# An encoder trunk on one core: a fourteenth seven-product pair in each half of the down-projection, a fifth pair with stored weight sums, and smaller stored activation sums

## The chip, the cores and the metric

The kernel runs on 1 core of one Trainium2 chip. The metric is the device time of one execution in microseconds (us). A core has engines that run beside each other: PE (TensorE, matrix products; PEld is its weight loads), DVE (VectorE), ACT (ScalarE), POOL (GpSimd, here mostly an issuer of DMAs) and SP (SyncE, an issuer of DMAs). Each engine works through its own instructions in order and waits on semaphores for the others.

## The reference

`x` is 256 positions by 2048 columns, all in float32. A mixer (a gated MLP branch and a neighbourhood attention branch) comes first and is not touched here. Then comes the part that matters:

```python
def conv_ffn(x, g_norm, w_up, conv_k, conv_b, w_down):
    h = rms_norm(x, g_norm)
    up = h @ w_up                       # 2048 -> 2 * 5504
    ...
    gate, val = jnp.split(up, 2, axis=-1)
    return x + (jax.nn.silu(gate) * val) @ w_down     # 5504 -> 2048
```

followed by a last `rms_norm`.

## The kernel before

**Products.** A float32 product is made of three matmuls on operands split in a high and a low part (`triple`, L316 to L319: high times high, low times high, high times low). The weights come from memory in pieces (`wraw`, five buffers, loads on SP's queue at L145). ACT copies a piece to its high part (`whi`, L170) and DVE subtracts to get the low part (`wlo`, L171); four buffers each, so this runs at most some three pieces ahead of PE.

**Up.** The stage has 22 groups (here numbered 0 to 21). A group makes two blocks of 128 gate columns and the two matching value columns, in eight pieces; group 21 has one block of each. After a group, DVE and ACT add the bank halves (L1066, L1068), run the convolution and the gate (L1074 to L1087) and split the result into the activation tiles `ff["a"]`, a few pieces later, within the next group. Group f makes activation pair f: two blocks of 128 of the 5504 columns.

**Down.** It is done in two halves of 1024 output columns (`g_dn`, `wide` and `run_wide`). A half takes 43 pieces of 128 rows: 21 pairs and one single. A plain piece is four triples, so a pair is eight. For the pairs of `DOWN_QUADS` the eight are replaced by seven, in Strassen's manner: these need four blocks of sums of the activations (`act_blocks`: s3, n1, p2, s4) and sums of the weights. In the first step of such a pair run three triples, which need of the sums only the last block s4; in the second step run four, which need the other three blocks and the weight sums.

The activation sums are made once, in the group behind their own (`sums`, `sums_split`), written to memory by POOL from the tile `so`, and loaded by POOL (`stored`) before each half needs them. The weight sums are made by DVE and ACT when the pair comes (`weight_sums`, `weight_sums_split`), except for the pairs of `DOWN_SPLIT`: theirs are made in the up stage by a job (`split_ahead`: one load `tw`, four additions at L1298, two splits at L1303 and L1304, four writes) and loaded as four tiles h13, l13, h24, l24 (`split_read`, L1258). Such a pair's first piece needs only half its columns. A job that starts with group g adds in the last two pieces of group g and the first two of group g+1 and splits in group g+1.

**Order.** The order on each engine is written out by hand: `at(i, f)` puts f in front of piece i. The second argument pair of a split pair, (6, 6), says how many pieces ahead its loads are put. Inside `wide` that loop uses the name `lead`, so that after the first split pair of a half the activation sums of later pairs are put 6 pieces ahead, not 4.

Of the kernel before, what the change touches and what calls it, by code (L numbers as in the profile page):

```python
# [67 lines left out]
TURN_X2 = (13, 1)  # L68
Y_GAP = 224
PAD = 16  # L70
DOWN_PAIRS = (3, 5, 6, 7, 9, 10, 11, 13, 14, 15, 17, 18, 19)
DOWN_QUADS = (DOWN_PAIRS, (2, 4, 5, 6, 8, 9, 10, 12, 13, 14, 16, 17, 18))
DOWN_SPLIT = (6, 10, 14, 18)
DOWN_JOBS = ((1, 3), (5, 7), (9, 11), (13, 17))
FIN_AT = 36


# [1 line left out]
def trunk_kernel(ctx, tc, x, x_t, vecs, w_in, ln_g, ln_b, w_st, b_s, rpb, w_branch, w_out, w_up, w_down,  # L79
# [109 lines left out]
    def at(i, f):  # L189
        tasks.setdefault(i, []).append(f)  # L190
# [160 lines left out]
    def sums_of(o):  # L351
        return [(o[:, 0, n * 128:(n + 1) * 128], o[:, 1, n * 128:(n + 1) * 128]) for n in range(4)]
# [187 lines left out]
    def split_plain(p, dst):  # L540
        nc.scalar.activation(dst[:, 0, :], p, AF.Copy)
        nc.vector.tensor_sub(dst[:, 1, :], p, dst[:, 0, :].bitcast(F32))
# [513 lines left out]

    ff = {}

    def ev_up(f0, nb):
        def done(ps, i):  # L1060
            n = nb
            a = []
            own = {}
            for p in ps:
                t = turns["p"].tile([128, T], F32, name="tb", bufs=3)
                nc.scalar.activation(t, p[:, T:], AF.Copy)  # L1066
                u = turns["p"].tile([128, T], F32, name="ta", bufs=6)
                nc.vector.tensor_add(u, p[:, :T], t)  # L1068
                a.append(u)

            def conv(b):
                c = []
                for u, ch in ((a[b], f0 + b), (a[n + b], NF + f0 + b)):
                    nc.vector.tensor_mul(u, u, rs["rb"])  # L1074
                    v = ff["p"].tile([128, T], F32, name="tc", bufs=4)
                    nc.scalar.activation(v, u, AF.Identity, scale=ck[:, 1, ch:ch + 1], bias=ck[:, 3, ch:ch + 1])  # L1076
                    c.append((u, v, ch))
                for u, v, ch in c:
                    nc.vector.scalar_tensor_tensor(v[:, 1:], u[:, :T - 1], ck[:, 0, ch:ch + 1], v[:, 1:],  # L1079
                                                   op0=OP.mult, op1=OP.add)  # L1080
                    nc.vector.scalar_tensor_tensor(v[:, :T - 1], u[:, 1:], ck[:, 2, ch:ch + 1], v[:, :T - 1],
                                                   op0=OP.mult, op1=OP.add)
                at(cur[0] + 1, lambda: gate(b, c[0][1], c[1][1]))

            def gate(b, g, v):
                nc.scalar.activation(g, g, AF.Silu)  # L1086
                nc.vector.tensor_mul(g, g, v)  # L1087
                at(cur[0] + 1, lambda: split_plain(g, ff["a"][f0 + b]))
                own[b] = g
                if b and f0 // 2 in ff["kept"]:  # L1090
                    at(cur[0] + 2, sums)
                    at(cur[0] + 3, sums_split)

            def sums():
                own["w"] = ff["more"].tile([128, 512], F32, name="sw")
                act_blocks(own["w"], *(own[k][:, t * 128:(t + 1) * 128] for k in range(2) for t in range(2)))

            def sums_split():
                o = ff["more"].tile([128, 2, 512], F32R, name="so")
                split_plain(own["w"], o)  # L1100
                nc.gpsimd.dma_start(ff["kept"][f0 // 2], o.bitcast(F32))

            at(i + 1, lambda: conv(0))
            if n > 1:
                at(i + (5 if f0 + 3 == NF else 3), lambda: conv(1))
        return done
# [285 lines left out]
    def down_room(name, dt):  # L1392
        return hpool.tile([128, 2, 512], dt, name=h_room[name])

    def stored(pair, box):
        n = ff["turn"] = (ff.get("turn", -1) + 1) % 3
        o = ff["twice"].tile([128, 2, 512], F32R, name="s2") if n == 2 else down_room(f"s{n}", F32R)
        nc.gpsimd.dma_start(o.bitcast(F32), ff["kept"][pair])
        box["s"] = sums_of(o)

    def down_split_tile(pair, name):
        return ff["twice"].tile([128, 2, 512], F32R, name=name)
# [3 lines left out]
    def down_order(g):  # L1406
# [4 lines left out]

    g_dn = [wide(w_d, 0, down_order(g), g * 1024, lambda k: ff["a"][k], DOWN_QUADS[g], down_room,
                 (ev_sums(2 * g, down_room), ev_down if g == 0 else finish), stored=stored,
                 split=({p: (6, 6) for p in DOWN_SPLIT}, split_read(d_kept, g, down_split_tile))) for g in range(2)]
    ff["kept"] = {p: dram.tile([128, 2, 512], F32, name=f"sums{p}") for p in DOWN_PAIRS}
    for p, turn in zip(DOWN_SPLIT, DOWN_JOBS):
        for g in range(2):
            d_kept[p, g] = split_rows("down", p, g)
# [100 lines left out]
    ctx.push(fa_st)  # L1519
    ff["ap"] = [fa.tile([128, min(2, NF - k), 2, T], F32R, name=f"a{k // 2}") for k in range(0, NF, 2)]  # L1520
    ff["a"] = [ff["ap"][k // 2][:, k % 2] for k in range(NF)]
    turns["p"], turns_st = pool("turns2")
    ff["more"], more_st = pool("more")
    fc = {}

    def open_conv():
        ff["p"], fc["st"] = pool("conv", "right")

    at(g_up[0][1] + 3, open_conv)
    for g in g_up:  # L1530
        run_group(g)
    def open_twice():
        more_st.close()
        turns_st.close()
        ff["twice"], twice_st = pool("twice")
        ctx.push(twice_st)

    at(g_dn[0][1] + 3, open_twice)

    def open_fin():  # L1540
        fc["st"].close()
# [56 lines left out]
```

## Time and profile before

| | us |
|---|---|
| median of 3 runs (1289.42 to 1290.4) | 1289.85 |
| the profiled execution's own time | 1290.33 |
| its span in the trace | 1288.5 |
| PE busy | 1277.2 |
| DVE busy | 1118.3 |
| ACT busy | 793.0 |
| POOL busy | 162.1 |

The span is the time from the first to the last instruction of the trace. Busy time is the union of an engine's instructions; matmuls overlap each other, so PE busy throughout does not tell by itself how fast matmuls follow each other. In times below, 1062.6 is the start of the down stage and 1171 that of its second half.

### The profile page before, as it was taken

The page shows a single profiled execution, that of the slowest core. Times are in us where ns is not written, and L with a number is a line of the kernel's source. Part 1 is how long each engine was busy: PE and PEld are TensorE (multiplying, and loading weights), DVE is VectorE, ACT ScalarE, POOL GpSimd, SP SyncE. Part 2 cuts the span into 40 slices and gives each one's busy share as a digit, 9 for nine tenths or more (in the row PEclk, how much of TensorE's full clock was granted, in tenths as well). Part 3 has the DMA queues.
Part 4 walks back from the last instruction along what each step waited for, and adds up shares of the span by engine and source line. Part 5 has one row for each costly group of instructions (what it writes and reads, how often), then busy time and mean ns, then how long its engine had stood idle before and what let it go on. Part 6 is the DMA issues. An engine that isn't in the chain of part 4 may idle for free.

```text
span 1288.5 us, 19673 instructions
## 1 busy us (share of the span) xinstructions
PE 1277.2 (99%) x6717; PEld 1088.7 (84%) x6717; DVE 1118.3 (87%) x1644; ACT 793.0 (62%) x1179; POOL 162.1 (13%) x307
## 2 busy tenths in 40 slices
PE   9999999999999999999999999999999999999997
PEld 7888888888887888888888888888888888888885
DVE  7898977777799989996889999998988989979987
ACT  7776575775755655565665666665665656556654
POOL 0003852330000001100001000100000001211210
PEclk9999999999999999999999999999999999999999
DMA  9789889989789977965688789888776859998993
GB/s 364 278 272 284 288 263 345 341 284 321 247 314 360 347 238 262 387 215 179 193 281 286 239 275 304 272 260 291 261 227 219 279 174 359 374 387 321 353 392 132
DMA packets 199893, 369.51 MB, mean 287 GB/s; under 512 B 15984, under 2 KB 124144, under 8 KB 199792
## 3 DMA queue, kind: packets, MB, share of 16 engines
q1 hardware_dynamic: 175472, 286.36, 64.7%
q0 software_dynamic: 23888, 81.23, 17.7%
q8 instruction: 52, 0.85, 0.2%
q10 hardware_dynamic: 432, 0.66, 0.1%
q14 instruction: 49, 0.40, 0.1%
HBM read 320.48 MB, written 45.61 MB: 284 GB/s over the span
## 4 chain that ended last, share of the span: by engine, by line
PE 96%; DVE 2%; DMA 1%; issue 1%; DVEq 0%; ACT 0%; SPq 0%; ACTq 0%
PE bank L222 31%; PE bank L226 16%; PE bank L319 11%; PE bank L317 11%; PE bank L318 11%; PE bank L250 5%; PE bank L251 5%; PE bank L252 5%; DMA wraw<-in_w_down_dram 1%; DVE wlo L171 1%; PE bank L871 0%; PE bank L825 0%; PE bank L498 0%; PE bank L860 0%; PE bank L698 0%
## 5 line engine op out<-in xcount | busy, mean ns | idle before, releaser
L171 DVE TENSOR_TENSOR wlo<-wraw,whi 128x1024 fp32r<-128x1024 f32 (+1 forms) x472 | 537.4, 1152 | 125.0 <-ACT whi L170 74.8
L170 ACT ACTIVATE whi<-wraw 128x1024 fp32r<-128x1024 f32 (+1 forms) x472 | 463.8, 995 | 224.1 <-PE bank L318 65.1
L222 PE MATMUL bank<-h,whi 128*128 128x512 f32 x1760 | 423.3, 391 | 0.0
L222 PEld LDWEIGHTS bank<-h,whi 128*128 128x128 f32 x1760 | 322.7, 188 | 62.1
L226 PEld LDWEIGHTS bank<-h,wlo 128*128 128x128 f32 x1760 | 225.9, 191 | 8.8
L226 PE MATMUL bank<-h,wlo 128*128 128x256 f32 x1760 | 228.6, 283 | 0.0
L1076 ACT ACTIVATE tc<-ta,ck 128x256 f32<-128x256 f32 x86 | 47.1, 595 | 109.8 <-DVE ta L1074 109.8
L319 PE MATMUL bank<-wlo,a 128*128 128x512 f32 x188 | 73.4, 390 | 0.6 <-DVE wlo L171 0.6
L318 PE MATMUL bank<-whi,a 128*128 128x512 f32 x188 | 73.2, 389 | 0.0
L317 PE MATMUL bank<-whi,a 128*128 128x512 f32 x188 | 73.1, 389 | 0.0
L317 PE MATMUL bank<-whi,h 128*128 128x512 f32 x186 | 72.8, 392 | 0.0
L319 PE MATMUL bank<-wlo,h 128*128 128x512 f32 x186 | 72.6, 390 | 0.0
L318 PE MATMUL bank<-whi,h 128*128 128x512 f32 x186 | 72.6, 390 | 0.0
L1079 DVE SCALAR_TENSOR_TENSOR tc<-ta,ck,tc 128x255 f32<-128x255 f32 x86 | 41.4, 482 | 14.4 <-ACT tc L1076 14.4
L250 PE MATMUL bank<-whi,h 128*128 128x512 f32 x128 | 50.3, 393 | 0.0
L250 PE MATMUL bank<-whi,y 128*128 128x512 f32 x128 | 50.3, 393 | 0.0
L251 PE MATMUL bank<-whi,h 128*128 128x512 f32 x128 | 49.8, 389 | 0.0
L251 PE MATMUL bank<-whi,y 128*128 128x512 f32 x128 | 49.8, 389 | 0.0
L252 PE MATMUL bank<-wlo,h 128*128 128x512 f32 x128 | 49.8, 389 | 0.0
L252 PE MATMUL bank<-wlo,y 128*128 128x512 f32 x128 | 49.8, 389 | 0.0
L374 ACT ACTIVATE h<-h 128x1024 fp32r<-128x1024 f32 x36 | 38.1, 1059 | 17.5 <-DVE h L364 12.0
L1308 POOL DMA_DIRECT2D down_h<-so x16 | 8.7, 544 | 311.2 <-ACT tc L1086 184.9
(325 smaller groups left out, 1990.1 us busy)
## 6 DMA issues: line engine op xcount, KB each, us to landing
wraw<-in_w_up_dram SPq DMA_DIRECT2D x336, 256.0 KB, 4.1
wraw<-in_w_in_dram SPq DMA_DIRECT2D x107, 512.0 KB, 6.1
wraw<-in_w_down_dram SPq DMA_DIRECT2D x78, 512.0 KB, 7.5
wraw<-in_w_in_dram SPq DMA_DIRECT2D x70, 256.0 KB, 4.4
wraw<-in_w_branch_dram SPq DMA_DIRECT2D x32, 512.0 KB, 5.3
wraw<-in_w_out_dram SPq DMA_DIRECT2D x28, 512.0 KB, 5.9
h<-sums POOLq DMA_DIRECT2D x18, 512.0 KB, 7.5
tw<-in_w_down_dram POOLq DMA_DIRECT2D x8, 1024.0 KB, 8.9
```

Source lines behind the costliest of these rows:

```text
L170: nc.scalar.activation(h[:, k, :m], w[:, k, :m], AF.Copy)
L171: nc.vector.tensor_sub(l[:, k, :m], w[:, k, :m], h[:, k, :m].bitcast(F32))
L222: nc.tensor.matmul(p, h[:, k - k0, b * 128:(b + 1) * 128], acts(k), start=k == 0, stop=k == nk - 1)
L226: nc.tensor.matmul(p[:, :T], l[:, k - k0, b * 128:(b + 1) * 128], acts(k)[:, 0, :], start=False, stop=False)
L250: nc.tensor.matmul(p, xh, h[:, kk, :m], start=st, stop=False)
L251: nc.tensor.matmul(p, xl, h[:, kk, :m], start=False, stop=False)
L252: nc.tensor.matmul(p, xh, l[:, kk, :m], start=False, stop=sp)
L317: nc.tensor.matmul(p, xh, h, start=st, stop=False, **kw)
L318: nc.tensor.matmul(p, xl, h, start=False, stop=False, **kw)
L319: nc.tensor.matmul(p, xh, l, start=False, stop=sp, **kw)
L1076: nc.scalar.activation(v, u, AF.Identity, scale=ck[:, 1, ch:ch + 1], bias=ck[:, 3, ch:ch + 1])
L1079: nc.vector.scalar_tensor_tensor(v[:, 1:], u[:, :T - 1], ck[:, 0, ch:ch + 1], v[:, 1:], op0=OP.mult, op1=OP.add)
```

## The change

`DOWN_PAIRS` gets pair 2, so that each half has fourteen seven-product pairs in place of thirteen (in the first half as the third pair, in the second half as the second). Pair 2 is also put in `DOWN_SPLIT`; the jobs now start with groups 1 to 19, every second one, two for each of five pairs. Of the activation sums only three blocks go through memory (384 columns high and low in place of 512). The fourth, s4, is written into a quarter of the pair's own activation tile that neither half reads any more (`fourth`). For that, one ACT and one DVE instruction of 512 columns become two each, of 384 and 128. The pools are laid out anew: the tiles for the loaded weight sums (`twice`) open three pieces before the down stage, and the third place for activation sums has a pool of its own.

```diff
-DOWN_PAIRS = (3, 5, 6, 7, 9, 10, 11, 13, 14, 15, 17, 18, 19)
-DOWN_QUADS = (DOWN_PAIRS, (2, 4, 5, 6, 8, 9, 10, 12, 13, 14, 16, 17, 18))
-DOWN_SPLIT = (6, 10, 14, 18)
-DOWN_JOBS = ((1, 3), (5, 7), (9, 11), (13, 17))
+DOWN_PAIRS = (2, 3, 5, 6, 7, 9, 10, 11, 13, 14, 15, 17, 18, 19)
+DOWN_QUADS = (DOWN_PAIRS, (1, 2, 4, 5, 6, 8, 9, 10, 12, 13, 14, 16, 17, 18))
+DOWN_SPLIT = (2, 6, 10, 14, 18)
+DOWN_JOBS = ((1, 3), (5, 7), (9, 11), (13, 15), (17, 19))
+DOWN_LEADS = ({2: (3, 6, 6)}, {})
...
+    def three(t):
+        return t.rearrange("p a b -> p (a b)")[:, :768].rearrange("p (a b) -> p a b", a=2)
+
+    def fourth(pair, n):
+        return ff["ap"][pair][:, 0, n, 128:]
...
             def sums_split():
-                o = ff["more"].tile([128, 2, 512], F32R, name="so")
-                split_plain(own["w"], o)
+                w = own["w"]
+                o = three(ff["more"].tile([128, 2, 512], F32R, name="so"))
+                nc.scalar.activation(o[:, 0], w[:, :384], AF.Copy)
+                nc.scalar.activation(fourth(f0 // 2, 0), w[:, 384:], AF.Copy)
+                nc.vector.tensor_sub(o[:, 1], w[:, :384], o[:, 0].bitcast(F32))
+                nc.vector.tensor_sub(fourth(f0 // 2, 1), w[:, 384:], fourth(f0 // 2, 0).bitcast(F32))
                 nc.gpsimd.dma_start(ff["kept"][f0 // 2], o.bitcast(F32))
...
     def stored(pair, box):
         n = ff["turn"] = (ff.get("turn", -1) + 1) % 3
-        o = ff["twice"].tile([128, 2, 512], F32R, name="s2") if n == 2 else down_room(f"s{n}", F32R)
+        if n == 2:
+            o = ff["third"].tile([128, 2, 384], F32R, name="s2")
+        else:
+            o = three(down_room(f"s{n}", F32R))
         nc.gpsimd.dma_start(o.bitcast(F32), ff["kept"][pair])
-        box["s"] = sums_of(o)
+        box["s"] = [(o[:, 0, n * 128:(n + 1) * 128], o[:, 1, n * 128:(n + 1) * 128]) for n in range(3)]
+        box["s"].append((fourth(pair, 0), fourth(pair, 1)))
...
-                 split=({p: (6, 6) for p in DOWN_SPLIT}, split_read(d_kept, g, down_split_tile))) for g in range(2)]
-    ff["kept"] = {p: dram.tile([128, 2, 512], F32, name=f"sums{p}") for p in DOWN_PAIRS}
+                 split=({p: DOWN_LEADS[g].get(p, (6, 6)) for p in DOWN_SPLIT}, split_read(d_kept, g, down_split_tile))) for g in range(2)]
+    ff["kept"] = {p: dram.tile([128, 2, 384], F32, name=f"sums{p}") for p in DOWN_PAIRS}
...
-    turns["p"], turns_st = pool("turns2")
+    fc = {}
+    ff["p"], fc["st"] = pool("conv", "right")
+    turns["p"], turns_st = pool("turns2", "right")
     ff["more"], more_st = pool("more")
...
+    at(g_dn[0][1] - 3, open_twice)
+    at(g_dn[0][1] + 3, open_third)
```

Two places of the order are shown, each before and after the change. The line numbers of the changed kernel are 1 higher around L171, 7 around L1068 and 11 around L1298.

The first place is POOL at the end of the up stage and the start of the first down half. `sums19` is the write of the last activation sums; h6, h7 and s2 are the three places for loaded sums; the name after `<-` tells the pair, so `down_h13_6_0` is the high part of one half of pair 6's weight sums for the first half. Before:

```order
L1101 DMA sums19_170<-so_11155 128x1024
L1398 DMA h6_11410<-sums3_158 128x1024
L1398 DMA h7_11507<-sums5_159 128x1024
L1398 DMA s2_11509<-sums6_160 128x1024
L1258 DMA h13_11511<-down_h13_6_0_171 128x1024
L1258 DMA l13_11512<-down_l13_6_0_172 128x1024
L1258 DMA h24_11515<-down_h24_6_0_173 128x1024
L1258 DMA l24_11516<-down_l24_6_0_174 128x1024
L1398 DMA h6_11570<-sums7_161 128x1024
```

After:

```order
L1112 DMA sums19_171<-so_11231 128x768
L1269 DMA h13_11401<-down_h13_2_0_172 128x1024
L1269 DMA l13_11402<-down_l13_2_0_173 128x1024
L1269 DMA h24_11405<-down_h24_2_0_174 128x1024
L1269 DMA l24_11406<-down_l24_2_0_175 128x1024
L1412 DMA h6_11450<-sums3_159 128x768
L1412 DMA h7_11474<-sums2_158 128x768
L1412 DMA s2_11562<-sums5_160 128x768
L1412 DMA h6_11601<-sums6_161 128x768
L1269 DMA h13_11603<-down_h13_6_0_180 128x1024
L1269 DMA l13_11604<-down_l13_6_0_181 128x1024
L1269 DMA h24_11607<-down_h24_6_0_182 128x1024
```

Four loads for pair 2 now stand right behind the last write of the up stage, and pair 6's loads stand behind sums that go into h6, where pair 3's sums lie.

The second place is DVE from the end of group 19 into group 20, the last full group of the up stage. Before:

```order
L325 TENSOR_TENSOR sw<-sw,tc 128x128
L326 TENSOR_TENSOR sw<-tc,sw 128x128
L171 TENSOR_TENSOR wlo<-wraw,whi 128x1024
L542 TENSOR_TENSOR so<-sw,so 128x512
L1068 TENSOR_TENSOR ta<-bank,tb 128x256 x4
L171 TENSOR_TENSOR wlo<-wraw,whi 128x1024 x2
L1074 TENSOR_TENSOR ta<-ta,rb 128x256 x2
```

After:

```order
L326 TENSOR_TENSOR sw<-sw,tc 128x128
L327 TENSOR_TENSOR sw<-tc,sw 128x128
L172 TENSOR_TENSOR wlo<-wraw,whi 128x1024
L1309 TENSOR_TENSOR tw<-tw 128x512
L1110 TENSOR_TENSOR so<-sw,so 128x384
L1111 TENSOR_TENSOR a_6045<-sw,a_6045 128x128
L1075 TENSOR_TENSOR ta<-bank,tb 128x256 x4
L172 TENSOR_TENSOR wlo<-wraw,whi 128x1024
L1309 TENSOR_TENSOR tw<-tw 128x512
L172 TENSOR_TENSOR wlo<-wraw,whi 128x1024
L1309 TENSOR_TENSOR tw<-tw 128x512
L1081 TENSOR_TENSOR ta<-ta,rb 128x256 x2
```

Additions of a job now stand between the weight splits here; two splits of the same job (`tw<-tw,so 128x1024`) follow further on in group 20, where there were none.

## Rows read from the trace of the kernel before

**Rows 1.** The page: PE's share, and the chain that ended last.
```profile
PE 1277.2 (99%) x6717; PEld 1088.7 (84%) x6717; DVE 1118.3 (87%) x1644; ACT 793.0 (62%) x1179; POOL 162.1 (13%) x307
...
PE 96%; DVE 2%; DMA 1%; issue 1%; DVEq 0%; ACT 0%; SPq 0%; ACTq 0%
```

**Rows 2.** Timeline of PE, first down half, pair 6: start us, us, instruction.
```profile
1096.14 0.39 PE L317 MATMUL bank<-h,s 128*128 128x512 f32 x1
1096.37 0.39 PE L318 MATMUL bank<-h,s 128*128 128x512 f32 x1
1096.59 0.39 PE L319 MATMUL bank<-l,s 128*128 128x512 f32 x1
...
1097.95 0.39 PE L319 MATMUL bank<-l,s 128*128 128x512 f32 x1
```

**Rows 3.** Timeline of DVE: first bank reads behind groups 6, 7, 8, 18, 20.
```profile
742.04 1.08 DVE L1068 TENSOR_TENSOR ta<-bank,tb 128x256 f32<-128x256 f32 x3
...
763.12 1.08 DVE L1068 TENSOR_TENSOR ta<-bank,tb 128x256 f32<-128x256 f32 x3
...
786.57 0.75 DVE L1068 TENSOR_TENSOR ta<-bank,tb 128x256 f32<-128x256 f32 x2
...
1009.24 1.41 DVE L1068 TENSOR_TENSOR ta<-bank,tb 128x256 f32<-128x256 f32 x4
...
1051.38 1.42 DVE L1068 TENSOR_TENSOR ta<-bank,tb 128x256 f32<-128x256 f32 x4 [0.26 <-ACT tb L1066]
```

**Rows 4.** Timeline of DVE, group 20: a long and a short weight split.
```profile
1044.01 1.22 DVE L171 TENSOR_TENSOR wlo<-wraw,whi 128x1024 fp32r<-128x1024 f32 x1
...
1045.48 0.69 DVE L171 TENSOR_TENSOR wlo<-wraw,whi 128x512 fp32r<-128x512 f32 x1
```

**Rows 5.** Timeline of DVE and PE around the start of the down stage.
```profile
1054.01 0.69 DVE L171 TENSOR_TENSOR wlo<-wraw,whi 128x512 fp32r<-128x512 f32 x1 [0.48 <-PE bank L226]
...
1060.52 1.23 DVE L171 TENSOR_TENSOR wlo<-wraw,whi 128x1024 fp32r<-128x1024 f32 x1 [0.25 <-ACT whi L170]
...
1064.59 1.22 DVE L171 TENSOR_TENSOR wlo<-wraw,whi 128x1024 fp32r<-128x1024 f32 x1
...
1065.86 0.50 PE L319 MATMUL bank<-wlo,a 128*128 128x512 f32 x1
```

**Rows 6.** Two windows: length, engines' busy us, granted clock, DMA share, GB/s.
```profile
1052.50:1065.00 12.50, 12.50 (x72) 10.93 (x71) 10.84 (x22) 8.15 (x15) 1.07 (x2) 1.00 0.87 255
1082.50:1097.50 15.00, 15.00 (x68) 12.39 (x67) 14.93 (x19) 9.49 (x11) 1.06 (x2) 1.00 0.90 317
```

**Rows 7.** DMA queues (packets, MB, share), and issues (count, KB, median us to landing).
```profile
q0 software_dynamic: 23888, 81.23, 17.7%
...
wraw<-in_w_down_dram SPq DMA_DIRECT2D x78, 512.0 KB, 7.5
...
l<-down_l POOLq DMA_DIRECT2D x16, 512.0 KB, 11.2
```

**Rows 8.** Timeline of SP and POOL: three DMA issues.
```profile
1053.55 0.34 SPq L145 DMA_DIRECT2D wraw<-in_w_down_dram  x1
...
1051.66 0.53 POOL L1101 DMA_DIRECT2D sums<-so  x1 [21.45 <-DVE so L542]
...
1083.68 0.53 POOL L1398 DMA_DIRECT2D h<-sums  x1 [7.55 <-PE bank L319]
```

**Rows 9.** Timeline of DVE and PE near the end.
```profile
1257.06 0.69 DVE L364 TENSOR_TENSOR h<-wraw 128x512 f32<-128x512 f32 x1 [1.13 <-DMA wraw<-in_w_down_dram]
...
1270.19 1.22 DVE L171 TENSOR_TENSOR wlo<-wraw,whi 128x1024 fp32r<-128x1024 f32 x1
...
1270.44 0.39 PE L318 MATMUL bank<-whi,a 128*128 128x512 f32 x1
1271.46 0.50 PE L319 MATMUL bank<-wlo,a 128*128 128x512 f32 x1 [0.63 <-DVE wlo L171]
1271.80 0.39 PE L317 MATMUL bank<-whi,a 128*128 128x512 f32 x1
```

**Rows 10.** Timeline of PE and DVE where the second down half starts.
```profile
1170.94 0.39 PE L317 MATMUL bank<-whi,a 128*128 128x512 f32 x1
...
1172.19 2.48 DVE L1114 TENSOR_TENSOR x<-bank,x 128x512 f32<-128x512 f32 x4
```

More of the change, by code (lines that the diff above doesn't have):

```diff
@@ L1521, in trunk_kernel, with open_twice, open_third @@
     ff["a"] = [ff["ap"][k // 2][:, k % 2] for k in range(NF)]
-    turns["p"], turns_st = pool("turns2")
+    fc = {}
+    ff["p"], fc["st"] = pool("conv", "right")
+    turns["p"], turns_st = pool("turns2", "right")
     ff["more"], more_st = pool("more")
[L1524 to L1529, printed above, removed]
+    def open_twice():
+        more_st.close()
+        ff["twice"], twice_st = pool("twice")
+        ctx.push(twice_st)
+    def open_third():
+        turns_st.close()
+        ff["third"], third_st = pool("third")
+        ctx.push(third_st)
+    at(g_dn[0][1] - 3, open_twice)
+    at(g_dn[0][1] + 3, open_third)
     for g in g_up:
         run_group(g)
[L1532 to L1538, printed above, removed]
     def open_fin():
```

## The prediction

> **What bounds the kernel now.** I read the page first: PE is busy for 99% of the span and makes 96% of the chain that ended last [rows 1]. So nearly all of the time is the sum of PE's matmuls, and a change can gain in two ways only: fewer matmuls, or the removal of one of the few waits in which PE stands. Then I read PE's timeline in the down stage to see how fast matmuls follow each other. In [rows 2] each lasts 0.39 us but starts 0.226 us behind the one before (eight steps from 1096.14 to 1097.95 us): they overlap, and the price of one is the step, not its duration. The granted clock is 1.00 in both windows of [rows 6], so these are steps at the upper level, 2.4 GHz.
>
> Third, I looked for PE's waits in the two places where the change has anything to do. At the start of the down stage there is almost none: the matmul at 1065.86 is the first that uses the low part of the second down piece, and DVE finishes that part (1064.59 + 1.22 = 1065.81) at the very moment it is wanted [rows 5]. The reader should keep this: reserve there is nil, and whatever makes DVE later at 1060 makes PE later by as much. Near the end there is a real wait: one matmul starts 1.02 us behind the one before, in place of 0.23, and the next 0.34 behind that, together 0.9 us lost, for a low part that DVE starts at 1270.19 [rows 9]. DVE's timeline, followed back from there, is closed up to 1257.06, where DVE had stood 1.13 us for a weight piece. So this last wait comes from a late load.
>
> **What is removed.** In each half one pair takes seven triples in place of eight: 2 x 3 = 6 matmuls. Nothing else on PE changes. 6 x 0.226 = 1.36 us. Had one taken the duration, 6 x 0.39 = 2.34 us, one would have counted the overlap twice. The Trainium skill (TensorE: Matmul & The Clock Gate, Back-to-back issue gap) gives for a sustained stream of weight loads and matmuls of 512 columns about 131 ns for each; by it the six would be worth 0.79 us. The rows here show 226 ns, and the measurement decides.
>
> **What is added in the up stage.** DVE gets the sums of pair 2, two more jobs, and in each of fourteen pairs two small instructions in place of one. The fixed part of one more instruction is about 2 x 0.69 - 1.22 = 0.16 us, an estimate from [rows 4]. While PE has a reserve this costs nothing: whi and wlo are made some three pieces ahead. How far DVE falls behind in a group that has both a job's splits and sums is seen in [rows 3]: from the first bank read behind group 7 to that behind group 8 DVE needs 786.57 - 763.12 = 23.45 us, while the two groups 7 and 8 take 786.57 - 742.04 = 44.53, so 22.27 each. DVE loses 1.2 us in such a group and has it back after the next, and PE does not stand for it. The job that moves to group 15 repeats this pattern, which the jobs at groups 3 to 13 have already, so I price all of that at zero; the cover is the three pieces, and without it each such group would cost PE 1.2 us.
>
> The exception is group 20, because behind it comes only the half-size group 21, and then the place without reserve. Group 20 now gets a job. Worked out: group 19 starts its DVE work at 1009.24 + 0.16, takes as long as group 7 did (763.12 - 742.04 = 21.08, sums and two additions) + 0.16, so it ends at 1030.64. Group 20 takes 23.45, less 3 x 0.53 because its last three weight pieces are short (1.22 against 0.69 [rows 4]), plus 0.16: 22.02. The read behind it starts at 1052.66 in place of 1051.38, 1.28 us later. On the way to the down stage DVE has 0.26 us idle already counted, 0.48 at 1054.01 and 0.25 at 1060.52 [rows 3, 5]. The 0.48 is a wait for PE and swallows lag; the 0.25 is a wait for ACT, whose copies hang on DVE's results, so it swallows little. That leaves a lag of 0.5 to 0.8 us at 1060.52, and as reserve is nil PE pays it. I take 0.6; bounds 0 (if ACT lets go earlier) and 1.3.
>
> **What is moved: the loads.** Pair 2's four loads of 0.52 MB now go out behind the last write of sums, at 1051.66 [rows 8]: two at once, two when that write has landed. The first piece of down weights is issued at 1053.55 [rows 8] and its copy by ACT ends before 1060.52 [rows 5]. The engines that carry POOL's queue spend 0.177 x 1288.5 / 81.23 = 2.81 us for each MB [rows 7], so 2.1 MB are 5.9 us; between 1052.5 and 1065 the DMA engines stand idle for 0.13 x 12.5 = 1.6 us [rows 6]. At worst the raw pieces land 4.3 us later. At best not at all, since loads issued earlier may be through. As nearest case I take the median of 7.5 us to landing for down pieces [rows 7], most of which are loaded beside such loads: 1053.55 + 7.5 = 1061.05, about 0.9 us past the moment at which ACT, itself later by the lag, would take the piece up (1060.52 + 0.6 - 1.06 for the copy, a little over 1060.0). I take half of it, 0.5, because only part of the loads meets the first piece.
>
> Pair 6 of the first half is the second place. Its sums now go into h6 and wait until PE is through with pair 3. That release is in the trace: 1083.68 [rows 8], today of pair 7's sums. Its four weight loads follow at steps of about 0.52 us, the last at 1085.8; with the median of 11.2 [rows 7] it lands at 1097.0, and PE wants it at 1097.95 [rows 2]. The DMA engines are 0.90 busy there without these loads [rows 6]. I take 0.2 us; bounds 0 and 1.2.
>
> In the second half pair 2's loads have some 20 us, and the raw pieces land far ahead: zero. Its four banks are wanted at the third piece, 24 matmuls behind 1170.94, so at 1176.4; DVE empties the banks of the first half from 1172.19 to 1174.7 [rows 10]. 1.7 us in hand: zero.
>
> **What the smaller sums give.** Each load of sums shrinks by 0.13 MB, three of them in each round of about 20 us: 0.39 x 2.81 = 1.1 us of DMA time. Near the end, where DVE stood 1.13 us for a load, part of this comes back. I take 0.5 us of the 0.9; bounds 0 and 0.9.
>
> **The sum.** -1.36 + 0.6 + 0.5 + 0.2 - 0.5 = -0.56. From the profiled execution's 1290.33 that gives 1289.8. That execution lies 0.48 above the median of the runs shown, 1289.85, so I forecast **1289.3 us**. No change and this differ by less than 0.2% (2.6 us), which is about what a measurement of this kernel can tell from no change.
>
> **The rivals.**
> Forecast: part of the saving is lost where the down stage starts, net 0 to -1.2. Chance 0.55.
> First: nothing new is waited for. Then -1.36 remains, and with the last wait gone -1.36 - 0.9 = -2.26: 1287.6 to 1288.5. For it: loads go out early, and total DMA in the down stage falls. Against: reserve at 1065.86 is nil. Chance 0.28.
> Second, on the other side: the raw pieces starve behind pair 2's loads. Place: the first three down pieces. If all 5.9 us of loads go ahead of them, PE stands up to 4.3 us, and with the lag and pair 6 the sum is +3.2, so 1293.1. It decides from 3.9 us of new stall on (1.36 + 2.6). For it: both loads are issued before the first raw piece. Against: it takes strict precedence, while pieces and loads mix at other places of the down stage without PE standing. Chance 0.12, of which 0.08 slower. The Trainium skill (DMA: Bandwidth & Descriptors, Queues, rings and completion order) says that each DMA engine goes round between the queues that have work, a packet at a time; by that neither queue starves, and a piece waits for about as many packets as it has itself. No row here shows single packets.
> Third: the banks of the second half are not free in time. If DVE were more than 1.7 us later there, PE would stand for the excess, at most about a microsecond: 1290.3. Chance 0.05.
>
> **How the numbers follow.** Faster by over 0.2% would need -2.6, more than the saving and both waits together can give (-2.4), so only spread of the runs can do it: 0.05. Slower by over 0.2%: 0.09. Within: 0.86. The range runs from the whole saving with the last wait gone, less a little, to the sum with the upper bound of the lag and half that of the loads (-1.36 + 1.3 + 2.15 + 0.2 - 0.5 = +1.8): 1287.5 to 1291.6.
>
> **What would show it.** Right: six matmuls fewer, at steps of 0.226; DVE's first bank read behind group 20 about 1.3 us later against the end of that group; a low part of the second down piece that PE waits for by about a microsecond; POOL's loads of pair 2 ahead of the first down piece; a smaller last wait. Wrong: PE standing in the up stage, pair 6's last load landing over a microsecond late, or a new wait in the second half where the trace of before has none.

## The result, and the profile after

The changed kernel takes 1293.34 us (median of 11 runs, 1291.91 to 1296.66), the kernel before beside it 1289.85 (11 runs). The ratio is 1.0029, 95% interval 1.0021 to 1.0037: slower by 0.29%, 3.5 us, and outside the predicted range. Its profiled execution took 1294.65 us, with a span of 1292.9 against 1288.5.

Its page, for [rows 1] and [rows 7]:

```profile
PE 1278.6 (99%) x6711; PEld 1088.6 (84%) x6711; DVE 1128.0 (87%) x1675; ACT 796.7 (62%) x1198; POOL 174.2 (13%) x328
...
q0 software_dynamic: 24480, 87.78, 19.2%
...
PE 94%; DVE 2%; DMA 2%; issue 1%; ACT 0%; POOL 0%; DVEq 0%; ACTq 0%
PE bank L223 30%; PE bank L227 15%; PE bank L320 11%; PE bank L318 11%; PE bank L319 11%; PE bank L251 5%; PE bank L252 4%; PE bank L253 4%; DMA l<-down_l 1%; DVE wlo L172 1%; DMA wraw<-in_w_down_dram 1%; PE bank L872 0%; PE bank L826 0%; PE bank L499 0%; PE bank L861 0%
```

There are six matmuls fewer, yet the chain that ended last (followed back from the last instruction, at each step to what it waited for) now has PE at 94% in place of 96%, and two transfers in it by name: the weight-sum tiles `l<-down_l` and the raw down pieces. To find where the time went I took, over the whole trace, the amount by which each start of a matmul lies further behind the one before than its usual step (0.226 us for 512 columns). Up to the end of the up stage the two kernels agree but for 0.14 us (its last matmul starts at 1062.39 before and at 1062.25 now), and between 640 and 1058 nothing is lost in either. Three places remain. In the first, where the down stage starts, PE loses 2.82 us (before 0.16). In the second, at 1100, it loses 3.83 (before nothing). The last wait is 0.57 (before 0.90). With the six matmuls that is -1.36 + 2.66 + 3.83 - 0.33 = +4.8, against +4.4 between the spans; the difference is the 0.14 just named and the stretch from the last matmul to the end, which takes 8.4 us in place of 8.8.

**Start of the down stage.** Timeline of ACT, DVE, PE, POOL and SP, for [rows 3, 5, 8]; in brackets, how long the engine stood and for whom:

```profile
1059.19 0.62 ACT L171 ACTIVATE whi<-wraw 128x512 fp32r<-128x512 f32 x1
1061.97 1.06 ACT L171 ACTIVATE whi<-wraw 128x1024 fp32r<-128x1024 f32 x1 [2.15 <-DMA wraw<-in_w_down_dram]
...
1052.23 1.41 DVE L1075 TENSOR_TENSOR ta<-bank,tb 128x256 f32<-128x256 f32 x4
...
1063.06 1.23 DVE L172 TENSOR_TENSOR wlo<-wraw,whi 128x1024 fp32r<-128x1024 f32 x1 [2.52 <-ACT whi L171]
1064.20 0.76 DVE L1081 TENSOR_TENSOR ta<-ta,rb 128x256 f32<-128x256 f32 x2
...
1067.13 1.22 DVE L172 TENSOR_TENSOR wlo<-wraw,whi 128x1024 fp32r<-128x1024 f32 x1
...
1063.08 0.50 PE L318 MATMUL bank<-whi,a 128*128 128x512 f32 x1 [0.43 <-ACT whi L171]
...
1064.34 0.50 PE L320 MATMUL bank<-wlo,a 128*128 128x512 f32 x1 [0.53 <-DVE wlo L172]
...
1068.40 0.50 PE L320 MATMUL bank<-wlo,a 128*128 128x512 f32 x1 [0.92 <-DVE wlo L172]
...
1053.61 0.54 POOL L1269 DMA_DIRECT2D h<-down_h  x1 [0.64 <-DMA down_l<-tw]
1054.13 0.54 POOL L1269 DMA_DIRECT2D l<-down_l  x1
1057.38 0.53 POOL L1269 DMA_DIRECT2D h<-down_h  x1 [2.71 <-DMA sums<-so]
...
1054.40 0.34 SPq L146 DMA_DIRECT2D wraw<-in_w_down_dram  x1
```

Read upwards from the last PE row: PE stands for the low part of the second piece; DVE starts that at 1067.13, behind the gate's work of group 21, which it takes up only after the first piece's low part at 1063.06; that waited 2.52 us for ACT's copy, and the copy 2.15 for the first raw piece. It was issued at 1054.40 and landed at about 1061.9, 7.5 us later, against 5.0 in the kernel before (both rows from the list of DMA issues, the kernel before first):

```profile
wraw<-in_w_down_dram SPq DMA_DIRECT2D x1, 512.0 KB, 5.0
...
wraw<-in_w_down_dram SPq DMA_DIRECT2D x1, 512.0 KB, 7.5
```

DVE's first bank read behind group 20 (1052.23) comes 10.0 us ahead of the start of the up stage's last matmul (1062.25); before it came 11.0 ahead (1051.38 [rows 3], 1062.39). So the lag is 1.0 us, and against the same mark the issue of the raw piece moved by 1.0 us too (1054.40, before 1053.55 [rows 8]).

**Pair 6.** Timeline of POOL and PE in the first half, for [rows 2, 8]:

```profile
1085.56 0.54 POOL L1412 DMA_DIRECT2D h<-sums  x1 [13.91 <-PE bank L320]
...
1087.67 0.53 POOL L1269 DMA_DIRECT2D l<-down_l  x1
...
1099.85 0.40 PE L319 MATMUL bank<-h,h 128*128 128x512 f32 x1
1101.95 0.77 PE L320 MATMUL bank<-l,h 128*128 128x512 f32 x1 [1.71 <-DMA l<-down_l]
1102.53 0.63 PE L318 MATMUL bank<-h,a 128*128 128x512 f32 x1
1102.95 0.63 PE L319 MATMUL bank<-h,a 128*128 128x512 f32 x1
...
1105.48 0.40 PE L319 MATMUL bank<-whi,a 128*128 128x512 f32 x1
1105.71 0.39 PE L320 MATMUL bank<-wlo,a 128*128 128x512 f32 x1
```

The window around it, for [rows 6] (the last three numbers are granted clock, DMA share and GB/s):

```profile
1099.00:1106.00 7.00, 5.29 (x16) 3.65 (x15) 5.82 (x6) 3.55 (x4) 2.66 (x5) 0.76 1.02 417
```

The load at 1085.56 is that of pair 6's activation sums, waiting for PE to finish pair 3; the fourth weight-sum tile goes out at 1087.67 and lands at 1101.9, 14.2 us later; PE wanted it at 1100.08. The rows for the last tile of such a group of four, from the list of DMA issues: pair 6 and pair 10 in the kernel before, then pair 6 here:

```profile
l<-down_l POOLq DMA_DIRECT2D x1, 512.0 KB, 10.7
...
l<-down_l POOLq DMA_DIRECT2D x1, 512.0 KB, 13.3
...
l<-down_l POOLq DMA_DIRECT2D x1, 512.0 KB, 14.2
```

Behind this wait of 1.9 us the matmuls start 0.43 us apart, not 0.23: the granted clock of the window is 0.76, so part of it is at the lower level, 1.2 GHz.

### The profile page after: what moved, and what is told of

The parts are those of the page before. It is cut to its first block, busy times and chain, and to the rows that moved or that the text cites. A ratio compares the mean times of both kernels' runs of the same rounds, so it can differ in the third digit from the quotient of the medians.

```text
span 1292.9 us, 19786 instructions
## 1 busy us (share of the span) xinstructions
PE 1278.6 (99%) x6711; PEld 1088.6 (84%) x6711; DVE 1128.0 (87%) x1675; ACT 796.7 (62%) x1198; POOL 174.2 (13%) x328
## 4 chain that ended last, share of the span: by engine, by line
PE 94%; DVE 2%; DMA 2%; issue 1%; ACT 0%; POOL 0%; DVEq 0%; ACTq 0%
PE bank L223 30%; PE bank L227 15%; PE bank L320 11%; PE bank L318 11%; PE bank L319 11%; PE bank L251 5%; PE bank L252 4%; PE bank L253 4%; DMA l<-down_l 1%; DVE wlo L172 1%; DMA wraw<-in_w_down_dram 1%; PE bank L872 0%; PE bank L826 0%; PE bank L499 0%; PE bank L861 0%
## 5 line engine op out<-in xcount | busy, mean ns | idle before, releaser
L171 ACT ACTIVATE whi<-wraw 128x1024 fp32r<-128x1024 f32 (+1 forms) x472 | 461.6, 993 | 224.0 <-PE bank L319 79.0
L320 PE MATMUL bank<-wlo,a 128*128 128x512 f32 x204 | 80.0, 392 | 1.7 <-DVE wlo L172 1.7
L318 PE MATMUL bank<-whi,a 128*128 128x512 f32 x204 | 80.0, 392 | 0.4 <-ACT whi L171 0.4
L319 PE MATMUL bank<-whi,a 128*128 128x512 f32 x204 | 79.6, 390 | 0.0
L318 PE MATMUL bank<-whi,h 128*128 128x512 f32 x168 | 66.0, 393 | 0.0
L319 PE MATMUL bank<-whi,h 128*128 128x512 f32 x168 | 65.6, 390 | 0.0
L320 PE MATMUL bank<-wlo,h 128*128 128x512 f32 x168 | 65.5, 390 | 0.0
L1309 DVE TENSOR_TENSOR tw<-tw 128x512 f32<-128x512 f32 x72 | 50.2, 697 | 0.7
L251 PE MATMUL bank<-whi,h 128*128 128x512 f32 x128 | 50.3, 393 | 0.0
L252 PE MATMUL bank<-whi,h 128*128 128x512 f32 x128 | 49.8, 389 | 0.0
L253 PE MATMUL bank<-wlo,h 128*128 128x512 f32 x128 | 49.8, 389 | 0.0
```

The source lines that it names most:

```text
L171: nc.scalar.activation(h[:, k, :m], w[:, k, :m], AF.Copy)
L251: nc.tensor.matmul(p, xh, h[:, kk, :m], start=st, stop=False)
L252: nc.tensor.matmul(p, xl, h[:, kk, :m], start=False, stop=False)
L253: nc.tensor.matmul(p, xh, l[:, kk, :m], start=False, stop=sp)
L318: nc.tensor.matmul(p, xh, h, start=st, stop=False, **kw)
L319: nc.tensor.matmul(p, xl, h, start=False, stop=False, **kw)
```

## The experiments

The twelve ran in three groups of four, each group on one chip together with the kernel before. A median is that of 11 runs, but of 6 for the changed kernel again and of 2 for experiment 8. In the table, a loss is the sum of late starts in us as above, and "landing" is the time from issue to landing of the first raw down piece; both are from the one profiled execution.

| kernel | median us | before | ratio, 95% interval | landing | loss at 1058 to 1075 | loss at 1075 to 1110 | last wait |
|---|---|---|---|---|---|---|---|
| before | 1289.85 | | | 5.0 | 0.16 | 0 | 0.90 |
| changed | 1293.34 | 1289.85 | 1.0029 (1.0021 to 1.0037) | 7.5 | 2.82 | 3.83 | 0.57 |
| changed again | 1293.68 | 1289.99 | 1.0031 (1.0019 to 1.0042) | 7.5 | 2.84 | 1.67 | 0.24 |
| 1: pair 6's loads first | 1291.96 | 1290.21 | 1.0015 (1.0006 to 1.0024) | 7.6 | 2.95 | 0.11 | 0.79 |
| 2: and jobs one group earlier | 1290.37 | 1290.21 | 0.9998 (0.9989 to 1.0007) | 7.5 | 1.86 | 0 | 0.71 |
| 3: 1, and half of pair 2's loads later | 1290.58 | 1290.21 | 1.0004 (0.9996 to 1.0013) | 7.4 | 2.73 | 0 | 0.16 |
| 4: small sums alone | 1289.57 | 1290.21 | 0.9992 (0.9983 to 1.0001) | 4.7 | 0.16 | 0 | 0.86 |
| 4 again | 1289.48 | 1290.18 | 0.9994 (0.9985 to 1.0003) | 4.8 | 0.17 | 0 | 0 |
| 5: no load of pair 2 near the first piece | 1287.77 | 1289.99 | 0.9981 (0.9973 to 0.9990) | 4.0 | 0.17 | 0 | 0.28 |
| 5 again | 1287.99 | 1290.18 | 0.9983 (0.9974 to 0.9992) | 4.6 | 0.16 | 0 | 0.55 |
| 6: 2 and 3 together | 1288.74 | 1289.99 | 0.9991 (0.9982 to 1.0000) | 6.4 | 0.79 | 0 | 0.51 |
| 7: 1, and all four loads later | 1289.61 | 1289.99 | 0.9999 (0.9990 to 1.0008) | 5.4 | 0.72 | 1.38 | 0 |
| 8: 5, and two tiles of pair 6 late | 1296.47 | 1290.18 | 1.0048 (1.0030 to 1.0067) | | 0.16 | 9.65 | 0 |
| 9: 5, with large sums | 1288.21 | 1290.18 | 0.9983 (0.9974 to 0.9991) | | 0.16 | 0 | 0.68 |

**The changed kernel again** (no edit).

> The changed kernel once more, unaltered, beside the next three on one chip. Its profiled execution was 1.3 us above the median of its runs. If the wait for pair 6's last tile and the stretch at the lower clock behind it are of one size in every execution, this profile shows about 3.8 us there again; if the wait is near a limit and the clock falls only in some executions, it shows another size, between 1 and 4 us, and the first experiment's gain of 1.4 to 1.7 us between medians is what this place costs as a rule.

The start loses the same 2.8 us; pair 6 loses less, and the clock does not fall behind its wait (PE's timeline):

```profile
1100.57 0.39 PE L319 MATMUL bank<-h,h 128*128 128x512 f32 x1
1102.10 0.50 PE L320 MATMUL bank<-l,h 128*128 128x512 f32 x1 [1.15 <-DMA l<-down_l]
1102.44 0.40 PE L318 MATMUL bank<-h,a 128*128 128x512 f32 x1
1102.67 0.40 PE L319 MATMUL bank<-h,a 128*128 128x512 f32 x1
```

The same window as above:

```profile
1099.00:1106.00 7.00, 5.85 (x26) 4.52 (x25) 6.59 (x7) 4.49 (x6) 2.65 (x5) 1.00 1.02 418
```

So pair 6's price differs from one execution to the next: 1.4 us in this one, 3.8 in the first. Which is the rule two profiles cannot tell; the medians of the next experiment speak for the smaller one.

**1. Pair 6's loads ahead of its sums on POOL's queue.**

```diff
-DOWN_LEADS = ({2: (3, 6, 6)}, {})
+DOWN_LEADS = ({2: (3, 6, 6), 6: (5, 6, 6)}, {})
```

> One edit to the changed kernel: in the first half the four weight-sum loads of pair 6 stand ahead of its activation sums on POOL's queue, so they no longer wait behind a load that waits for PE to finish pair 3; they wait for pair 2's tiles only and should go out near 1081 in place of 1086.1. Theory (the price of the change lies in two separate places, and this place costs about 4.0 us: a wait of 1.9 us for the last of the four tiles, 0.6 of refills behind it, and about 1.4 us of matmuls at the lower clock): the wait at 1100 and the stretch at granted clock below 1 are gone, the median falls from 1293.3 to about 1289.4, and the spread of the single times shrinks, as the drop of the clock is no longer there. Rival (bandwidth, not order: the DMA engines are short of time until 1100): the loads, 5 us earlier, delay the raw pieces of 1080 to 1095, PE waits there instead, and the median stays above 1291.5.

The loads went out at 1080.55 to 1082.43, and the wait at 1100 was gone. So the order was the cause: with the loads 5 us earlier PE loses only 0.11 us between 1075 and 1110, which is against the rival's mechanism. The median, though, missed the expected 1289.4 by 2.6 us and lies above the rival's mark of 1291.5. It stands 1.75 us above the kernel before, against 3.5 and 3.7 for the changed kernel: this place cost 1.7 to 1.9 us between medians, not 4.0, since I had put the bad case down as the rule. The spread did not shrink either (1290.78 to 1295.68).

**2. The jobs one group earlier as well.**

```diff
-DOWN_JOBS = ((1, 3), (5, 7), (9, 11), (13, 15), (17, 19))
+DOWN_JOBS = ((0, 2), (4, 6), (8, 10), (12, 14), (16, 18))
```

> The first experiment's order for pair 6, and the ten jobs each start one group earlier (groups 0 to 18 in place of 1 to 19), so that none works in group 20. Theory lag (DVE's lag out of group 20 makes the first raw down piece go out 0.85 us later, and that is part of the 2.8 us that PE loses at the start of the down stage): the first piece is issued at about 1053.5 again, PE loses about 2 us there in place of 2.8, and the median is 0.8 us below the first experiment. Theory loads (only the four loads of pair 2 ahead of the first raw piece count): they go out earlier by as much, the piece lands as late as before, and the median equals that of the first experiment within 0.3 us. If jobs and sums that fall together in fewer groups matter in the up stage, that shows there as well, at most 0.1 us.

The first piece goes out at 1053.50 again and the loss falls by 1.1 us to 1.86, as theory lag said; but its landing is still 7.5 us behind its issue. The median falls by 1.6 us, more than the expected 0.8; the profiles do not account for all of that.

**3. Half of pair 2's loads behind the loads of sums** (the leads of the others kept in the code of `wide`).

```diff
-DOWN_LEADS = ({2: (3, 6, 6), 6: (5, 6, 6)}, {})
+DOWN_LEADS = ({2: (3, 6, 3), 6: (5, 6, 6)}, {})
```

> The first experiment's order for pair 6, and of pair 2's four loads in the first half two (h24 and l24, half of the bytes) are put behind two loads of activation sums that wait for PE at 1062.3; the leads of all other loads are kept. Theory loads (the first raw down piece lands 3.3 us later than in the kernel before because it shares the DMA engines with pair 2's loads): with half of the bytes away in front of it, the first piece lands 1 to 1.5 us earlier, PE's loss at the start of the down stage falls from 2.8 to about 1.5 us, and the median is about 1.2 us below the first experiment. Theory lag: the loss stays near 2.8 us and the median equals that of the first experiment. A third outcome: the two late tiles land after 1077, when PE wants them, and the loss moves there.

A miss for theory loads as I had sized it: landing 7.4 us, loss 2.73, only 0.2 less. The median is 1.4 below the first experiment's, but by this profile 0.6 of that is the last wait. It is not that the loads don't count: with DVE's lag in place, the two that go out 0.8 and 0.3 us ahead of the raw piece are enough. The two moved here had gone out 2.1 and 2.6 us behind it in the first experiment.

**7. All four loads behind the loads of sums, lag left in.**

```diff
-DOWN_LEADS = ({2: (3, 6, 3), 6: (5, 6, 6)}, {})
+DOWN_LEADS = ({2: (3, 3, 3), 6: (5, 6, 6)}, {})
```

> Lag alone at the start of the down stage: the jobs as in the changed kernel, one of them in group 20, but all four loads of pair 2 behind the loads of sums at 1062; pair 6's order as in the first experiment. If lag alone had a price of 0.6 us or more, as the prediction has it, PE loses that at 1062 to 1068. By the chain in the changed kernel's trace (ACT is free for the first piece at 1059.8, 0.4 us later than before) it is 0.4 to 0.6 with the refills behind it. A loss of over 2 us there would speak against the loads. A second loss is expected at pair 2's second step, near 1077, of 0.5 to 2 us, since the last of its tiles is then issued only 12 us ahead.

With lag alone the loss at the start is 0.72 us, 0.56 more than the 0.16 of the kernel before, and of the 2.95 of the first experiment the other 2.2 are the loads' doing. The second loss came where it was expected, and without a fall of the clock. PE's waits between 1058 and 1110 (us in total, times, longest):

```profile
PE bank L321 <- DMA l<-down_l: 1.1, 1, 1.1
PE bank L321 <- DVE wlo L172: 0.4, 1, 0.4
```

**6. Jobs earlier, half of the loads later** (the edits of 2 and 3).

> Between the second experiment and the one just named: jobs one group earlier, h13 and l13 of pair 2 ahead of the first raw piece (issued near 1052), h24 and l24 behind the loads of sums. By theory loads the first raw piece lands 5.5 to 6.8 us behind its issue, between the 7.5 with four loads and the 5.0 with none, and PE loses 0.4 to 1.4 us at the start. If only the loads that are issued ahead of the raw piece count, this equals the second experiment: 7.5 us and 1.9.

6.4 us and 0.79: between, as theory loads said. The two landings:

```profile
wraw<-in_w_down_dram SPq DMA_DIRECT2D x1, 512.0 KB, 7.5
...
wraw<-in_w_down_dram SPq DMA_DIRECT2D x1, 512.0 KB, 6.4
```

The first is that of experiment 2. The two loads now go out 1.7 and 1.2 us ahead of the raw piece. In the second experiment two more follow 1.3 and 1.9 us behind it, and cost another 1.1 us: here a later load on POOL's queue delays a piece that went out on SP's before it. Two that followed 2.1 and 2.6 us behind it cost only 0.2 (experiment 1 less 3).

**5. No load of pair 2 near the first raw piece.** Its high and low tile of the first kind go into the jobs' tile `tw` in group 20; the others follow behind its sums, which now come first.

```diff
-DOWN_JOBS = ((1, 3), (5, 7), (9, 11), (13, 15), (17, 19))
-DOWN_LEADS = ({2: (3, 6, 6)}, {})
+DOWN_JOBS = ((0, 2), (4, 6), (8, 10), (12, 14), (16, 18))
+DOWN_LEADS = ({2: (3, 20, 3), 6: (6, 6, 6)}, {})
...
+    def first_read(pair, box, n):
+        u = box.setdefault("u", [])
+        if n == "13":
+            t = ff["more"].tile([128, 4, 512], F32R, name="tw")
+            u.append([t[:, :2], t[:, 2:]])
+            for v, src in zip(u[0], d_kept[pair, 0][n]):
+                nc.gpsimd.dma_start(v.bitcast(F32), src)
+            return
...
-    at(g_dn[0][1] - 3, open_twice)
-    at(g_dn[0][1] + 3, open_third)
+    tasks.setdefault(g_dn[0][1] + 6, [])[:0] = [open_twice, open_third]
```

> The jobs one group earlier, as in the second experiment, and no load of pair 2 near the first raw down piece: h13 and l13 are loaded in group 20 into the room of the jobs' own tile, which is free by then, h24 and l24 behind the first load of sums that waits for PE at 1062; the pools for the later tiles open six pieces into the half; pair 2's sums take the first place, so that pair 6's do not wait for pair 3. Theory loads (what is left of the loss at the start, 1.9 us in the second experiment, is the first raw piece landing 7.5 us behind its issue in place of 5.0): it lands within 5.5 us of its issue at 1053.5, PE loses 0.1 to 0.4 us at the start of the down stage, as before the change, there is no wait at 1100, and the median is 1.4 to 2 us below the second experiment, that is 0.8 to 1.4 us below the kernel before: ratio 0.9990 to 0.9994. Rival (the raw piece is late for another reason, for example that the stage's DMA traffic as a whole is too much): the loss at the start stays at 1.5 to 2 us or moves to pair 2's second step near 1077, and the median equals that of the kernel before.

Two of the loads go out in group 20; the first down piece lands 4.0 us behind its issue, DVE's row is that of [rows 5] again, with the idle time of before, and PE makes 98% of the chain. The page:

```profile
PE 1276.3 (99%) x6711; PEld 1088.1 (85%) x6711; DVE 1128.1 (88%) x1675; ACT 796.0 (62%) x1198; POOL 174.5 (14%) x329
...
PE 98%; DMA 1%; DVE 0%; issue 0%; ACT 0%; DVEq 0%; ACTq 0%
```

The timeline of POOL, DVE and PE:

```profile
1032.62 0.53 POOL L1428 DMA_DIRECT2D tw<-down_h  x1
...
1060.83 1.22 DVE L172 TENSOR_TENSOR wlo<-wraw,whi 128x1024 fp32r<-128x1024 f32 x1 [0.26 <-ACT whi L171]
...
1064.89 1.22 DVE L172 TENSOR_TENSOR wlo<-wraw,whi 128x1024 fp32r<-128x1024 f32 x1
...
1066.17 0.50 PE L321 MATMUL bank<-wlo,a 128*128 128x512 f32 x1
```

The median is 2.2 us below the kernel before, more than the 0.8 to 1.4 expected; this version beats both kernels. The second time:

> The kernel with pair 2's loads away from the first raw piece, unaltered, a second time and on the same chip as the next three. Expected: 2 us below the kernel before again, a ratio of about 0.998 with an interval that ends below 1.

It was 2.2 us again, ratio 0.9983.

**9. The same with large sums.** One place of the edit:

```diff
-                o = three(ff["more"].tile([128, 2, 512], F32R, name="so"))
-                nc.scalar.activation(o[:, 0], w[:, :384], AF.Copy)
-                nc.scalar.activation(fourth(f0 // 2, 0), w[:, 384:], AF.Copy)
-                nc.vector.tensor_sub(o[:, 1], w[:, :384], o[:, 0].bitcast(F32))
-                nc.vector.tensor_sub(fourth(f0 // 2, 1), w[:, 384:], fourth(f0 // 2, 0).bitcast(F32))
+                o = ff["more"].tile([128, 2, 512], F32R, name="so")
+                split_plain(own["w"], o)
```

> The kernel just named with the activation sums as they were before the change: all four blocks, 512 columns, through memory. This undoes the smaller sums alone, with fourteen pairs and no new wait. The prediction gave the smaller sums 0.5 us, in the last wait. If that is right, this kernel is 0.3 to 0.9 us slower than the one beside it and its last wait is 0.5 us longer, or new waits show at the start of the down stage, where three loads of sums then carry 0.39 MB more. If the smaller sums are worth nothing in time, the two agree within 0.3 us and the last wait is of the same size.

1288.21 against 1287.99 beside it, the last wait 0.68 against 0.55: the smaller sums are worth no more than 0.2 us, which these runs cannot tell from nothing.

**4. The smaller sums alone**, twice.

```diff
-DOWN_PAIRS = (2, 3, 5, 6, 7, 9, 10, 11, 13, 14, 15, 17, 18, 19)
+DOWN_PAIRS = (3, 5, 6, 7, 9, 10, 11, 13, 14, 15, 17, 18, 19)
```

(and the tables beside it as before the change).

> The smaller sums alone: thirteen seven-product pairs, four with stored weight sums, and the jobs as in the kernel before; three blocks of sums through memory and the fourth in the activation tile, pools laid out as in the changed kernel. Theory (the prediction's term for the smaller sums, 0.5 us of the last wait, is roughly right, and nothing else of the change hangs on them): the last wait falls from 0.9 to 0.4 to 0.6 us, no other wait is new, the median is 0.3 to 0.5 us below the kernel before. Rival (the two extra instructions of each pair or the new pools cost something where the down stage starts): PE waits at 1062 to 1068 and the median is 0.3 to 1 us above the kernel before.

> Thirteen pairs with the smaller sums, unaltered, a second time. Its last wait was 0.86 us in the first profile, as in the kernel before, against 0.0 to 0.8 in the profiles with fourteen pairs. If it is the fourteenth pair that shortens the last wait (it spares the subtraction of four plain pieces on the vector engine), the last wait here is 0.7 to 1.0 again and the time is within 0.5 us of the kernel before. If the smaller sums shorten it, it is below 0.6.

The median is 0.6 and 0.7 us below the kernel before, but both intervals take in 1, and experiment 9 gains as much beyond its six matmuls with large sums; so if there is a gain here, it is not shown to come from the smaller sums. The last wait was 0.86 us in one profile and 0 in the other, so it differs between executions of one kernel by as much as the whole term, and my inference that the fourteenth pair shortens it does not hold.

**8. Two tiles of pair 6 behind a load that waits for PE.**

```diff
-DOWN_LEADS = ({2: (3, 20, 3), 6: (6, 6, 6)}, {})
+DOWN_LEADS = ({2: (3, 20, 3), 6: (6, 6, -1)}, {})
```

> The same kernel with one wait put in on purpose: in the first half h24 and l24 of pair 6 go out behind a load of sums that waits for PE to finish pair 5, at about 1094, so that PE wants them at 1097 and 1098 and stands there some 5 us and then 2 more. In the changed kernel's first profile PE stood 1.9 us at that place and the next seven matmuls started 0.43 us apart, at a granted clock below 1; in its second profile PE stood 1.3 us and the steps stayed at 0.23. If the clock falls behind a longer wait, some matmuls behind this one start 0.43 us apart and the cost is the wait plus 1 us or more. If the first case was of another cause, the steps are 0.23 at once and the cost is the wait alone, 5 to 8 us.

PE's timeline there, and the window:

```profile
1096.36 0.39 PE L321 MATMUL bank<-l,h 128*128 128x512 f32 x1
1102.12 0.79 PE L319 MATMUL bank<-h,h 128*128 128x512 f32 x1 [5.36 <-DMA h<-down_h]
1102.71 0.63 PE L320 MATMUL bank<-h,h 128*128 128x512 f32 x1
1104.04 0.79 PE L321 MATMUL bank<-l,h 128*128 128x512 f32 x1 [0.70 <-DMA l<-down_l]
1104.63 0.63 PE L319 MATMUL bank<-h,a 128*128 128x512 f32 x1
1105.05 0.63 PE L320 MATMUL bank<-h,a 128*128 128x512 f32 x1
...
1109.32 0.48 PE L321 MATMUL bank<-wlo,a 128*128 128x512 f32 x1
1109.64 0.40 PE L319 MATMUL bank<-h,h 128*128 128x512 f32 x1
```

```profile
1096.00:1108.00 12.00, 5.94 (x15) 3.93 (x14) 4.71 (x5) 2.44 (x3) 2.63 (x5) 0.63 0.83 327
```

There are two waits, 5.5 and 1.1 us beyond the step, and behind them steps of 0.43 us until 1109: eleven, each 0.2 us above the usual, 2.2 us beside the waits. Between medians the late tiles cost 8.5 us (1296.47 against 1287.99, the first of only two runs). So the clock fell again behind a long wait, as in the changed kernel's first profile. The evidence is one profile of each kernel; in the other twelve no single wait is over 1.4 us, and none has such steps behind a wait.

## Why the prediction was wrong

**What held.** Six matmuls fewer, each 0.226 us: the kernel without new waits (5) gains 2.2 us, nearly the first rival's sum of 2.26. By the profiles 1.36 of it are the matmuls, 0.3 to 0.6 the last wait (0.28 and 0.55, before 0.90), and 0.3 the stretch behind the last matmul (8.4 us, before 8.8), which was in no sum. The up stage costs nothing: no late start between 640 and 1058 in any of the profiles, and in all of them PE takes 473.6 us from the last transpose of `x`, early in the stage, to the stage's last matmul. No banks are missing at the start of the second half: nothing is lost between 1168 and 1182. DVE's lag was forecast at 1.28 us and measured 1.0; its price alone was forecast at 0.6 and measured 0.56 (0.72 in experiment 7, less the 0.16 of before). The two places named were the two places that lost.

**The step that failed first** is "I take half of it, 0.5, because only part of the loads meets the first piece". Two things were wrong in it. The landing came 7.5 us after the issue, exactly the median that I had taken, so the whole of it counted, not half (and the whole, 1061.05 less a little over 1060.0, was 1.0 rather than 0.9). And I had added the lag to ACT's side alone, where it makes the wait look smaller; the same lag frees the raw buffers later, so the piece was also issued 1.0 us later, and POOL's loads moved onto it: they wait for the last write of the job in group 20, and the first went out at 1053.61 and not at 1051.66, 0.8 us ahead of the piece in place of 1.9. Lag and loads are no two terms that add: with the lag, two loads cost 2.0 us (experiment 3 less 7); without it the same two cost 0.6 (6 less 5). The term was 0.5 and measured 2.2. My upper bound of 4.3 held it, and so did the range, which had half of that, 2.15, and the lag at 1.3; these two terms alone would not have left it. Without pair 6's wait (experiment 1) the change stands at +1.75, just within the range's +1.8. The Trainium skill (DMA: Bandwidth & Descriptors, Queues, rings and completion order) says that each DMA engine goes round between the queues that have work, a packet at a time. Experiments 6 and 2 agree: neither queue starves, the piece lands 6.4 and 7.5 us behind its issue against 4.0 to 5.4 with no such load near it, and a load issued behind it still delays it.

**The second step that failed**, and the one that took the time out of the range, is pair 6's "I take 0.2 us; bounds 0 and 1.2". It measured 1.4 in one profile and 3.8 in the other, 1.7 to 1.9 between medians. The release came as worked out, as far ahead of PE's demand (14.5 us, forecast 14.3). What was off is the landing: I took the median of 11.2 us over all low tiles [rows 7], but the tile that PE waits for is the last of four that stand one behind the other, and these are slower than the median: 14.2 and 13.4 us here. The trace of before had such rows: pair 6's own last tile took 10.7 us, pair 10's 13.3, and those of the six other groups 12.0 to 15.0. Pair 10's loads go out from 1099.16, where the DMA engines are as full (1.01 from 1100 to 1125) as they are here (1.02 in the window from 1099). With 13.3 the forecast's own sum gives 1099.1 against 1097.95, so 1.1 us. The rest of the bad case, the fall of the clock, no row of before showed.

**The last term**, -0.5 for smaller sums in the last wait, has no support: experiment 9 undoes them and loses 0.2 us, which cannot be told from nothing, and experiment 4 has the wait once at 0.86 and once at 0.

Put together with what the runs gave, the sum is -1.36 + 0.56 + 2.2 + 1.7 to 1.9, so +3.1 to +3.3, against +3.5 and +3.7 between medians; the rest, some 0.4 us, is not accounted for.

**The second rival** named the right direction and nearly the time (1293.1), but by luck, since the sum was another: the loads gave 2.2 us and not 4.3, and pair 6, which it had at 0.2, gave the rest. Its condition, that the loads take strict precedence, was not needed.

What stays open: the spread of single runs of the changed kernel and of the first experiment (up to 1296.66 and 1295.68), since no profile is of the longest ones. Their mean granted clock is known: 0.996 or 0.997 in the four longest runs of the changed kernel, 0.998 or 0.999 in eleven of its thirteen others. So a fall of the clock may well be part of it, but not all: the first experiment has 0.996 in two runs near its median. Open is also what sets the last wait from one execution to the next. And up to 1.5 us of the difference between two profiles lies in the mixer, which no kernel here changes: that last transpose of `x` comes at 588.3 us in one profile and at 589.8 in another.

## What to carry to other kernels

Where a stage starts with no reserve, follow a delay on both sides of a wait: the engine that is late also frees buffers and issues loads later, and what used to miss a transfer may then meet it. For a tile that is loaded as one of several on a queue, take the time to landing of the last of such a group, not the median of them all. A new load is best put where the DMA engines have time (here 0.57 busy from 1025 to 1050 in the kernel before, 0.87 from 1052.5 [rows 6]). Here the same seven-product pair lost 0.29% as it was first placed, and gained 0.18% with two of its loads 21 us earlier and the others 6 us later, the jobs one group earlier, and pair 6's loads no longer behind pair 3.

## What the hardware showed that was not expected

A wait of PE can cost more than itself. Behind a wait of 1.9 us the next seven matmuls started 0.39 to 0.43 us apart (granted clock 0.76 in the 7 us around it), which added 1.4 us; behind one of 5.5 and one of 1.1 us it was eleven at 0.43 (granted clock 0.63), which added 2.2. Behind single waits of 1.3 us, in the second profile of the changed kernel and in experiment 7, the steps stayed at 0.23. Each case is one execution. And even a short wait has a tail: the step behind it was 0.31 to 0.34 in place of 0.23 us at the waits at the upper level.
